# Hybrid decoder layer: three visits a head pair in the mixer, scores, transposes and PV in one stretch, norms in the transposes' PSUM banks

## The chip, the cores and the metric

One core of a Trainium2 chip runs one launch of the kernel. The metric is the device time of that launch in microseconds (us). Three runs of the kernel before gave 1025.48, 1026.85 and 1027.06 us; the median is 1026.85.

The names used below: PE is TensorE (matmuls and transposes; PEld its weight loads), DVE is VectorE, ACT is ScalarE, POOL is GpSimd, SP the queue that issues the loads.

## The reference

One decoder layer on 512 tokens of width 1024, in float32: a half-step SwiGLU FFN, a token mixer, a second half-step FFN, each behind an RMSNorm that is scaled and shifted by a conditioning vector. The change touches the mixer alone. It has eight stick-breaking heads and eight forgetting (fox) heads of width 64:

```python
# stick-breaking, for each tile of 128 queries
z = einsum('bhqd,bhkd->bhqk', q[start:end], k[:end]) * scale
mask = arange(end)[None, :] < arange(start, end)[:, None]
log_keep = where(mask, log_sigmoid(-z), 0)
later = cumsum(log_keep, reverse=True) - log_keep
w = where(mask, exp(log_sigmoid(z) + later), 0);  out = w @ v
# forgetting, with q and k RMS-normed per head (gains g_q, g_k)
z = z + log_f_cum[start:end, None] - log_f_cum[None, :end]
p = softmax(where(mask, z, -inf));  out = p @ v
```

log_f_cum is a running sum of log_sigmoid of a per-head forget gate. The heads are concatenated and multiplied by w_o.

## The kernel before, in words

Activations are held transposed (features on the partitions, 512 tokens along the row), with the tokens in reverse order, so that query tile i sees the last 512 - 128 i columns: tile 0 has 512 columns of scores, tile 3 has 128. To keep float32 precision, each operand of a projection is split into a high and a low part (`prep`, lines 119 to 124: ACT casts hi, and another engine subtracts to get lo), and each product is three matmuls (`mm3`, lines 126 to 129).

PSUM has eight banks of 128x512: three named mm (projections), two z (scores), two pt (transposes) and one o (the output of PV), line 106. A bank is given to a new tile when the last reader of the old one is done.

The mixer handles heads in pairs, `ORDER = [4, 5, 6, 7, 0, 1, 2, 3]`: four fox pairs, then four stick-breaking pairs. A pair's way:

- `project` (line 743) makes q and k of the pair, 8 steps of one `mm3` each. For a fox pair, the lo part of the second weight tile is made on POOL, everything else on DVE.
- For a fox pair `norm_start` (755) squares them on ACT and POOL (`nsq`, `nsh`, `nsl`), and `norm_end` (763) multiplies by a block of ones (`bones`, two matmuls) into an mm bank `m`. ACT then does Ln, Exp and a square on it (`rsqrt2`, 148), and DVE reads the bank in line 152 (`nu`), makes `nr` (153) and scales q or k (768, `nq`). Only after line 152 is the bank free.
- `stacks` (800) lays out QH, QL and KS for the scores.
- `scores` (817) does the score matmuls of one query tile i for the two heads into two z banks and then `weigh` (841): for fox a maximum and its correction on DVE (`mx`, 847 and 848), Exp on ACT (`fw`), a reciprocal on DVE (853), and the scaling on POOL (854); for stick-breaking two sigmoids on ACT (`keep`, `beta`), a scan on DVE (`R`, 861), and a product on POOL (864).
- `transposed` (867) transposes one head's weights, 128 columns at a time, into a pt bank and copies them out to PT; `values` (880) multiplies them with V into the o bank (PV); `heads_out` (892) splits the result.

Between these PE runs "filler": the projections of later pairs, V's projections (lines 598 to 628) and the first part of the output projection (`o_proj`), 181 steps of three to six matmuls. PE's order is the order in which the program is written (`manual_schedule` for PE); the orders on DVE, ACT and POOL are chosen by the scheduler. `advance(n)` (955) emits filler until n steps are done, and after each step it pops one entry of `side`, where the norms and the stacks wait for their turn. A pair's two norms are popped at the fourth and fifth step of the next pair's projection.

The main loop (966 to 982) goes over 32 units (pair, tile). Unit u emits its scores, filler up to `target(2u)`, the first head's transposes of unit u-1, one more step of filler, PV of unit u-2, filler up to `target(2u+1)`, and the second head's transposes of u-1. `target` is 36 + 2.5 t until t = 52, and then grows by 1.125 a half unit.

Of the kernel before, what the change touches and what calls it, by code (L numbers as in the profile page):

```python
# [33 lines left out]
def hybrid_layer(  # L34
# [626 lines left out]
    nc.gpsimd.affine_select(
        out=free_sb[:, :P], in_=free_sb[:, :P], compare_op=ALU.is_gt, fill=1.0, base=0, pattern=[[1, P]],
        channel_multiplier=-1,
    )
    nc.gpsimd.memset(keep_sb, 1.0)
    nc.gpsimd.affine_select(
        out=keep_sb[:, :P], in_=keep_sb[:, :P], compare_op=ALU.is_gt, fill=0.0, base=0, pattern=[[-1, P]],
        channel_multiplier=1,
    )
# [4 lines left out]
    logf = mp.tile([P, 8, 8], F32, tag="logf", name="logf")[:, :4, :]  # L674
    nc.vector.tensor_scalar(fneg, fc, -1.0, 0.0, op0=ALU.mult, op1=ALU.add)
# [87 lines left out]
    def norm_end(q, sh, sl, col):  # L763
        m = bank("mm")
        nc.tensor.matmul(m, bones, sh, start=True, stop=False)
        nc.tensor.matmul(m, bones, sl, start=False, stop=True)
# [49 lines left out]

    def scores(p, i):
        while p not in ready:
            side.pop(0)()
        KS, QH, QL = ST[p]  # L820
        fox = p >= NPAIR
        n = S - i * P
        nn = max(n, 256)
        zs = [bank("z") for _ in range(2)]
        qsl, ksl = slice(i * P, (i + 1) * P), slice(S - nn, S)
        for g, z in enumerate(zs):
            nc.tensor.matmul(z[:, :nn], QH[:, g, qsl], KS[:, g, ksl], start=True, stop=False)
# [3 lines left out]
        if not fox:  # L831
            for g, z in enumerate(zs):
                a, _ = halves(g)
                nc.tensor.matmul(z[:, :nn], QL[a, 0, qsl], KS[a, g, ksl], start=False, stop=True)
        return [weights(p, g, i, z[:, nn - n : nn], n) for g, z in enumerate(zs)]

    def weights(p, g, i, z, n):
        with tc.high_priority(offset=200):
            return weigh(p, g, i, z, n)

    def weigh(p, g, i, z, n):
        if p >= NPAIR:
            hd = 2 * (p - NPAIR) + g
            mx = mp.tile([P, 1], F32, tag="mx", name=nm("mx"), bufs=4)
            sm = mp.tile([P, 1], F32, tag="sm", name=nm("sm"), bufs=4)
            lq = lfq[:, i, hd : hd + 1]
            nc.vector.tensor_reduce(mx, z, AX.X, ALU.max)
            nc.vector.scalar_tensor_tensor(
                out=mx, in0=mx, scalar=lq, in1=lq, op0=ALU.add, op1=ALU.subtract, reverse1=True
            )  # L850
            w = wt2k("fw")
            act(w[:, :n], z, AF.Exp, bias=mx, accum_out=sm)
            nc.vector.reciprocal(sm, sm)
            nc.gpsimd.tensor_scalar(w[:, :n], w[:, :n], sm, 0.0, op0=ALU.mult, op1=ALU.add)
            return w, n
# [8 lines left out]
        nc.gpsimd.tensor_tensor(beta[:, :n], beta[:, :n], R[:, :n], op=ALU.mult)
        return beta, n

    def transposed(p, g, w, n):
        pt = bank("pt")
# [3 lines left out]
        if p < NPAIR:  # L872
            nc.vector.tensor_tensor(PT[:, :n], pt[:, :n], keep_sb[:, :n], op=ALU.mult)
        elif g:
            nc.scalar.copy(PT[:, :n], pt[:, :n])
        else:
            nc.vector.tensor_copy(PT[:, :n], pt[:, :n])
        return PT

    def values(p, i, pts, ob):  # L880
        n = 4 - i
        for j in range(n):
            for g in range(2):
                nc.tensor.matmul(  # L884
                    ob[g * 64 : g * 64 + 64, i * P : (i + 1) * P],
                    V[:, i + j, (2 * p + g) * 64 : (2 * p + g + 1) * 64],
                    pts[g][:, j * P : (j + 1) * P],
                    start=j == 0,
                    stop=j == n - 1,
                )  # L890

# [70 lines left out]

    units = [(p, i) for p in ORDER for i in range(4)]
    with tc.manual_schedule(engines={ENG.PE}):
        advance(36)
        ws, pts, obs = {}, {}, {}
        for u in range(len(units) + 3):
            if u < len(units):
                ws[u] = scores(*units[u])
            for g in range(2):  # L970
# [12 lines left out]
        advance(1000)  # L983
# [112 lines left out]
```

## Time and profile before

| what | us |
|---|---|
| median of three runs | 1026.85 |
| the profiled execution | 1026.44 |
| its span, first to last instruction | 1024.7 |
| mean granted PE clock | 0.993 of full |
| PE busy | 1004.2 |
| DVE busy | 576.3 |
| ACT busy | 373.1 |
| POOL busy | 125.7 |

The mixer takes roughly the stretch from 400 to 640 us. In a timeline a row gives the start, the time it took, the engine, the line, and the operation with `out<-in`, the tiles by the program's names. A mark such as `[3.86 <-DVE KS L795]` says that the engine stood idle for 3.86 us before this row and that DVE's write of KS in line 795 ended that. The granted clock is the share of full speed at which PE was allowed to run. Durations of PE's rows overlap, since matmuls are pipelined: what one costs is read from its start to the start of the next.

### The profile page before, as it was taken

To read this page: it belongs to the slowest core of one execution; us is meant where nothing else is said; L and a number is where in the kernel's file an instruction comes from. 1 tells how busy PE (TensorE), PEld (TensorE's weight loads), DVE (VectorE), ACT (ScalarE), POOL (GpSimd) and SP (SyncE) were. 2 spreads that over 40 slices of the span, in tenths; PEclk is the share of its full clock that TensorE was granted. 3 is DMA by queue.
4 is the path that set the end of the run, shared out by engine and by line. 5 is a ranking of instruction groups with operands and counts; after the bars stand their busy time and mean duration, and the time that the engine had idled before them with its cause. 6 is when DMAs were issued, how large, how long until landed. Compare 5 with 4: busy or idle time off the path is not lost.

```text
span 1024.7 us, 13165 instructions
## 1 busy us (share of the span) xinstructions
PE 1004.2 (98%) x5148; PEld 832.9 (81%) x5148; DVE 576.3 (56%) x942; ACT 373.1 (36%) x600; POOL 125.7 (12%) x125
## 2 busy tenths in 40 slices
PE   7999999999999999989999999999999999999998
PEld 6788888888888899767787767998888888888887
DVE  4999989534333447699867675753333333333332
ACT  5343212322222325767556461542222232123220
POOL 1000000000000123345313355100000000000000
PEclk8999999999999999989999999999999999999999
DMA  8889899432222312301111111232323322332221
GB/s 310 296 316 329 320 323 334 170 90 101 103 102 79 128 51 75 119 26 54 70 63 59 46 42 62 83 103 103 97 89 103 102 81 87 107 110 89 90 76 60
DMA packets 37357, 129.38 MB, mean 126 GB/s; under 512 B 4272, under 2 KB 4528, under 8 KB 37296
## 3 DMA queue, kind: packets, MB, share of 16 engines
q1 hardware_dynamic: 35856, 126.40, 36.1%
q10 hardware_dynamic: 1440, 2.16, 0.6%
q8 instruction: 40, 0.66, 0.3%
q14 instruction: 21, 0.17, 0.0%
HBM read 126.44 MB, written 2.10 MB: 125 GB/s over the span
## 4 chain that ended last, share of the span: by engine, by line
PE 84%; DVE 7%; issue 3%; DMA 2%; ACT 2%; POOL 1%; SPq 0%; ACTq 0%; DVEq 0%; POOLq 0%
PE mm L127 10%; PE mm L128 10%; PE mm L129 10%; PE pt L128 7%; PE pt L129 7%; PE pt L127 7%; PE z L128 6%; PE z L127 6%; PE z L129 6%; DMA wm<-wmod 2%; PE o L884 2%; PE pt L870 2%; PE mm L398 1%; DVE junk L211 1%; PE mm L607 1%
## 5 line engine op out<-in xcount | busy, mean ns | idle before, releaser
L122 ACT CAST hi<-raw 128x1024 fp32r<-128x1024 f32 (+2 forms) x154 | 158.8, 1033 | 450.7 <-PE mm L128 143.6
L123 DVE TENSOR_TENSOR lo<-raw,hi 128x1024 fp32r<-128x1024 f32 (+2 forms) x149 | 181.0, 1217 | 131.3 <-ACT hi L122 125.5
L127 PE MATMUL mm<-hh,hi 128*128 128x512 f32 (+1 forms) x464 | 183.5, 395 | 0.5 <-DVE nu L152 0.5
L128 PE MATMUL mm<-hl,hi 128*128 128x512 f32 (+1 forms) x464 | 178.0, 384 | 0.1
L129 PE MATMUL mm<-hh,lo 128*128 128x512 f32 (+1 forms) x464 | 178.0, 384 | 0.0
L128 PE MATMUL pt<-al,hi 128*128 128x512 f32 (+1 forms) x331 | 128.1, 387 | 0.3 <-DVE al L451 0.3
L129 PE MATMUL pt<-ah,lo 128*128 128x512 f32 (+1 forms) x331 | 128.0, 387 | 0.0
L127 PE MATMUL pt<-ah,hi 128*128 128x512 f32 (+1 forms) x331 | 128.0, 387 | 0.0
L128 PE MATMUL z<-hl,hi 128*128 128x512 f32 (+1 forms) x336 | 127.3, 379 | 0.0
L129 PE MATMUL z<-hh,lo 128*128 128x512 f32 (+1 forms) x336 | 127.3, 379 | 0.0
L127 PE MATMUL z<-hh,hi 128*128 128x512 f32 (+1 forms) x336 | 127.3, 379 | 0.0
L127 PEld LDWEIGHTS mm<-hh,hi 128*128 128x128 f32 x464 | 87.7, 189 | 19.8 <-issue 3.6
L129 PEld LDWEIGHTS mm<-hh,lo 128*128 128x128 f32 x464 | 87.5, 189 | 17.4
L462 DVE SCALAR_TENSOR_TENSOR x<-pt,gcol,x 128x512 f32<-128x512 f32 (+1 forms) x51 | 36.4, 713 | 114.5 <-PE pt L129 114.5
L128 PEld LDWEIGHTS mm<-hl,hi 128*128 128x128 f32 x464 | 87.7, 189 | 15.1 <-DVE hl L167 0.3
L447 DVE TENSOR_TENSOR av<-sg,z 128x512 f32<-128x512 f32 x41 | 28.1, 686 | 105.3 <-PE z L129 105.3
L211 DVE SCALAR_TENSOR_TENSOR junk<-wm,c_bc 128x1024 f32<-128x1024 f32 x56 | 68.4, 1221 | 10.8 <-DMA wm<-wmod 10.4
L128 PEld LDWEIGHTS pt<-al,hi 128*128 128x128 f32 x331 | 62.1, 188 | 13.2 <-DVE al L451 0.7
L127 PEld LDWEIGHTS z<-hh,hi 128*128 128x128 f32 x336 | 63.2, 188 | 11.9
L129 PEld LDWEIGHTS z<-hh,lo 128*128 128x128 f32 x336 | 63.2, 188 | 11.8
L128 PEld LDWEIGHTS z<-hl,hi 128*128 128x128 f32 x336 | 63.2, 188 | 11.8
L127 PEld LDWEIGHTS pt<-ah,hi 128*128 128x128 f32 x331 | 62.2, 188 | 12.8
(296 smaller groups left out, 1433.8 us busy)
## 6 DMA issues: line engine op xcount, KB each, us to landing
raw<-w SPq DMA_DIRECT2D x80, 512.0 KB, 3.5
wm<-wmod SPq DMA_DIRECT2D x72, 512.0 KB, 6.0
raw<-wqk SPq DMA_DIRECT2D x16, 512.0 KB, 3.5
raw<-w1d SPq DMA_DIRECT2D x16, 448.0 KB, 3.3
raw<-w2d SPq DMA_DIRECT2D x16, 448.0 KB, 3.2
raw<-w1s SPq DMA_DIRECT2D x8, 512.0 KB, 6.9
raw<-w1d SPq DMA_DIRECT2D x8, 512.0 KB, 5.1
raw<-wo SPq DMA_DIRECT2D x8, 512.0 KB, 3.4
```

What stands on the lines that cost most here:

```text
L122: nc.scalar.copy(hi, raw)
L123: (lo_engine or nc.vector).tensor_tensor(lo, raw, hi.bitcast(F32), op=ALU.subtract)
L127: nc.tensor.matmul(ps, lh, rh, start=first, stop=False)
L128: nc.tensor.matmul(ps, lh, rl, start=False, stop=False)
L129: nc.tensor.matmul(ps, ll, rh, start=False, stop=last)
L211: nc.vector.scalar_tensor_tensor(out=junk, in0=wm, scalar=1.0, in1=c_bc, op0=ALU.mult, op1=ALU.mult, accum_out=mods[:, i : i + 1])
L398: nc.tensor.matmul(kb[j], lh if n < 2 else ll, h["l" if n == 1 else "h"][k], start=False, stop=k == KD - 1 and n == 2)
L447: nc.vector.tensor_tensor(av, sg, ps[1], op=ALU.mult)
L462: nc.vector.scalar_tensor_tensor(out=x[e][:, sl], in0=ps[:, sl], scalar=g_col(gm)[:, e : e + 1], in1=x[e][:, sl], op0=ALU.mult, op1=ALU.add)
L607: nc.tensor.matmul(b[:, :n], hh, wh, start=k == 0, stop=False)
L870: nc.tensor.transpose(pt[:, j * P : (j + 1) * P], w[:, j * P : (j + 1) * P], ident)
L884: nc.tensor.matmul(ob[g * 64 : g * 64 + 64, i * P : (i + 1) * P], V[:, i + j, (2 * p + g) * 64 : (2 * p + g + 1) * 64], pts[g][:, j * P : ...
```

## The change

The mixer goes over 24 visits instead of 32 units: for each pair tile 0, tile 1, and then tiles 3 and 2 together in one z bank each (`VISITS`). Per visit PE's order is now one stretch: scores of this visit, both heads' transposes of the visit before, PV of the visit before that. Filler comes only between stretches, up to `target(v)`: 36 + 20 v / 3, and from v = 19.5 on 3 steps a visit. Within fox scores the masks' matmuls come last. `norm_end` takes its bank from pt instead of mm. The lo part of the second weight tile of a fox pair is made on DVE instead of POOL. `free_sb` and `keep_sb` become 640 columns wide so that a merged visit finds a mask for two blocks; the merged fox visit does maximum, Exp, reciprocal and scaling for each of its two blocks, and the merged stick-breaking visit one scan, one product and two sigmoids over 384 columns a head. `fcol` and `logf` share a tile, and `mx` and `sm` share a tile with eight buffers.

The core of the diff:

```diff
-    def target(t):
-        return int(min(36 + 2.5 * t, 163 + 1.125 * (t - 52)))
+    def target(v):
+        return int(min(36 + 20 * v / 3, 163 + 3 * (v - 19.5)))
+
+    VISITS = ((0,), (1,), (3, 2))
...
-            wt = prep(wqk[2 * p + u], D, nc.gpsimd if fox and u else None)
+            wt = prep(wqk[2 * p + u], D)
...
     def norm_end(q, sh, sl, col):
-        m = bank("mm")
+        m = bank("pt")
...
+        def mm(z, sl, w, r, **kw):
+            nc.tensor.matmul(z[:, sl], w, r, skip_group_check=len(seg) > 1, **kw)
+
         for g, z in enumerate(zs):
-            nc.tensor.matmul(z[:, :nn], QH[:, g, qsl], KS[:, g, ksl], start=True, stop=False)
+            for n, (i, _, sl, qsl, ksl) in enumerate(parts):
+                mm(z, sl, QH[:, g, qsl], KS[:, g, ksl], start=n == 0, stop=False)
             if fox:
-                nc.tensor.matmul(z[:, :nn], QL[:, g, qsl], late[p % 2][:, g, ksl], start=False, stop=False)
-                nc.tensor.matmul(z[:, nn - n : nn - n + P], ident_b, mask_fx, start=False, stop=True)
...
+                for i, _, sl, qsl, ksl in parts:
+                    mm(z, sl, QL[:, g, qsl], late[p % 2][:, g, ksl], start=False, stop=False)
+        if fox:
+            for z in zs:
+                for i, n, sl, _, _ in parts:
+                    mm(z, slice(sl.stop - n, sl.stop - n + P), ident_b, mask_fx, start=False, stop=True)
+        else:
+            for i, _, sl, qsl, ksl in parts:
+                for g, z in enumerate(zs):
+                    a, _ = halves(g)
+                    mm(z, sl, QL[a, 0, qsl], KS[a, g, ksl], start=False, stop=True)
...
-    units = [(p, i) for p in ORDER for i in range(4)]
+    units = [(p, seg) for p in ORDER for seg in VISITS]
     with tc.manual_schedule(engines={ENG.PE}):
-        advance(36)
         ws, pts, obs = {}, {}, {}
-        for u in range(len(units) + 3):
+        for u in range(len(units) + 2):
+            advance(target(u))
             if u < len(units):
                 ws[u] = scores(*units[u])
-            for g in range(2):
-                advance(target(2 * u + g))
-                if 0 <= u - 1 < len(units):
-                    p, i = units[u - 1]
-                    pts[p, i, g] = transposed(p, g, *ws[u - 1][g])
-                if g == 0 and 0 <= u - 2 < len(units):
-                    advance(target(2 * u) + 1)
-                    p, i = units[u - 2]
-                    if i == 0:
-                        obs[p] = bank("o")
-                    values(p, i, (pts.pop((p, i, 0)), pts.pop((p, i, 1))), obs[p])
-                    if i == 3:
-                        heads_out(p, obs.pop(p))
+            if 0 <= u - 1 < len(units):
+                pts[u - 1] = [transposed(units[u - 1][0], g, *ws[u - 1][g]) for g in range(2)]
+            if 0 <= u - 2 < len(units):
+                p, seg = units[u - 2]
+                if seg == VISITS[0]:
+                    obs[p] = bank("o")
+                values(p, pts.pop(u - 2), obs[p])
+                if seg == VISITS[-1]:
+                    heads_out(p, obs.pop(p))
```

Three places of the instructions' order show what moved. First, PE at the norms of the last fox pair (`nsh`, `nsl` are the squares' parts, `mm_` and `pt_` the banks). Before, this stands between the norm of k and the next transposes:

```order
L765 MATMUL mm_4150<-nsh_4066,bones 128x512
L766 MATMUL mm_4150<-nsl_4067,bones 128x512
L127 MATMUL mm_4078<-hh_2834,hi_4073 128x512
L128 MATMUL mm_4078<-hl_2842,hi_4073 128x512
L129 MATMUL mm_4078<-hh_2834,lo_4074 128x512
L127 MATMUL mm_4078<-hh_2835,hi_4073 128x512
L128 MATMUL mm_4078<-hl_2843,hi_4073 128x512
L129 MATMUL mm_4078<-hh_2835,lo_4074 128x512
L870 MATMUL pt_4178<-ident,fw_4049 128x128 x2
```

and now the sixth visit (visit 5, counted from 0) follows the norm of k at once:

```order
L768 MATMUL pt_4062<-nsh_4023,bones 128x512
L769 MATMUL pt_4062<-nsl_4024,bones 128x512
L835 MATMUL z_4073<-KS_3659,QH_3660 128x256 x2
L835 MATMUL z_4073<-k_602_3360,QL_3661 128x256 x2
L835 MATMUL z_4074<-KS_3659,QH_3660 128x256 x2
L835 MATMUL z_4074<-k_602_3360,QL_3661 128x256 x2
L835 LDWEIGHTS ident_b
L835 MATMUL z_4073<-mask_fx,ident_b 128x128
...
L894 MATMUL pt_4113<-ident,fw_3977 128x128 x3
L894 MATMUL pt_4119<-ident,fw_3984 128x128 x3
```

The norm's tile is pt_4062 now, and pt_4119, the second head's transposes, is given the same bank; the transposes of the first head get the bank of q's norm.

Second, DVE at the same place (`mx` is the maximum of the scores `z`, `nu` the read that frees a norm's bank). Before, the two reads stand with one copy between them, and the next scores' maxima behind both:

```order
L152 SCALAR_TENSOR_TENSOR nu_4110<-mm_4106,nu_4110 128x512
L853 RECIPROCAL sm_4132<-sm_4132 128x1
L853 RECIPROCAL sm_4140<-sm_4140 128x1
L153 SCALAR_TENSOR_TENSOR nr_4109<-nu_4110,nr_4109 128x512
L768 SCALAR_TENSOR_TENSOR nq_3939<-nq_3939,gs,nr_4109 128x512
L877 COPY PT_4181<-pt_4178 128x256
L152 SCALAR_TENSOR_TENSOR nu_4154<-mm_4150,nu_4154 128x512
L781 TENSOR_TENSOR QL_4166<-nq_3939,QH_4165 64x512
L153 SCALAR_TENSOR_TENSOR nr_4153<-nu_4154,nr_4153 128x512
L847 TENSOR_REDUCE mx_4221<-z_4213 128x1
```

and now, with z_4073 and z_4074 the scores of visit 5:

```order
L152 SCALAR_TENSOR_TENSOR nu_4052<-pt_4048,nu_4052 128x512
L871 TENSOR_REDUCE mx_4088<-z_4073 128x1
L153 SCALAR_TENSOR_TENSOR nr_4051<-nu_4052,nr_4051 128x512
L872 SCALAR_TENSOR_TENSOR mx_4088<-mx_4088,lfq 128x1
L771 SCALAR_TENSOR_TENSOR nq_3890<-nq_3890,gs,nr_4051 128x512
L876 RECIPROCAL mx_4088<-mx_4088 128x1
L871 TENSOR_REDUCE mx_4094<-z_4073 128x1
L871 TENSOR_REDUCE mx_4101<-z_4074 128x1
L872 SCALAR_TENSOR_TENSOR mx_4094<-mx_4094,lfq 128x1
L872 SCALAR_TENSOR_TENSOR mx_4101<-mx_4101,lfq 128x1
L152 SCALAR_TENSOR_TENSOR nu_4066<-pt_4062,nu_4066 128x512
```

The read of k's bank pt_4062 stands behind three maxima of visit 5's own scores and a reciprocal that needs ACT's Exp of them. At visits 1 and 3 it stands behind that visit's two maxima in the same way (rows `mx_3712`, `mx_3719`, then `nu_3649`; `mx_3910`, `mx_3917`, then `nu_3863`).

Third, POOL ahead of the first scores (`fw`, the first of them, is the scaling of visit 0's weights). Before:

```order
L123 TENSOR_TENSOR lo_3411<-raw_3409,hi_3410 128x1024
L123 TENSOR_TENSOR lo_3547<-raw_3545,hi_3546 128x1024
L760 TENSOR_TENSOR nsl_3404<-nsq_3402,nsh_3403 128x512
L123 TENSOR_TENSOR lo_3712<-raw_3710,hi_3711 128x1024
L760 TENSOR_TENSOR nsl_3443<-nsq_3441,nsh_3442 128x512
L760 TENSOR_TENSOR nsl_3531<-nsq_3529,nsh_3530 128x512
L123 TENSOR_TENSOR lo_3956<-raw_3954,hi_3955 128x1024
L760 TENSOR_TENSOR nsl_3582<-nsq_3580,nsh_3581 128x512
L854 TENSOR_SCALAR fw_3629<-fw_3629,sm_3626 128x512
```

and now:

```order
L763 TENSOR_TENSOR nsl_3407<-nsq_3405,nsh_3406 128x512
L763 TENSOR_TENSOR nsl_3446<-nsq_3444,nsh_3445 128x512
L763 TENSOR_TENSOR nsl_3534<-nsq_3532,nsh_3533 128x512
L763 TENSOR_TENSOR nsl_3585<-nsq_3583,nsh_3584 128x512
L877 TENSOR_SCALAR fw_3628<-fw_3628,mx_3629 128x512
```

The four casts of 1024 columns are in DVE's queue now, each behind ACT's cast of its hi part.

More of the change, by code (lines that the diff above doesn't have):

```diff
@@ L587, in hybrid_layer @@
     V = mp.tile([P, 4, D], F32, tag="V", name="V")
-    fcol = mp.tile([P, 8, 8], F32, tag="fcol", name="fcol")[:, :4, :]
+    fl32 = mp.tile([P, 8, 8], F32, tag="fl32", name="fl32")
+    fcol, logf = fl32[:, :4, :], fl32[:, 4:, :]
     evn = [0]
@@ L656, in hybrid_layer @@
         nc.vector.memset(bones.bitcast(F32)[g * 64 : (g + 1) * 64, g * 64 : (g + 1) * 64], 1.0 / 64)
-    free_sb = mconst([P, S], BF16, "free_sb")
-    keep_sb = mconst([P, S], BF16, "keep_sb")
+    free_sb = mconst([P, S + P], BF16, "free_sb")
+    keep_sb = mconst([P, S + P], BF16, "keep_sb")
     nc.gpsimd.memset(free_sb, 0.0)
[L661 to L664, printed above, removed]
     nc.gpsimd.memset(keep_sb, 1.0)
[L666 to L669, printed above, removed]
+    for blk in (slice(0, P), slice(P, 2 * P)):
+        nc.gpsimd.affine_select(
+            out=free_sb[:, blk], in_=free_sb[:, blk], compare_op=ALU.is_gt, fill=1.0, base=0, pattern=[[1, P]],
+            channel_multiplier=-1,
+        )
+        nc.gpsimd.affine_select(
+            out=keep_sb[:, blk], in_=keep_sb[:, blk], compare_op=ALU.is_gt, fill=0.0, base=0, pattern=[[-1, P]],
+            channel_multiplier=1,
+        )
     fc = fcol.rearrange("p s e -> p (s e)")
@@ L815, in stacks, with scores @@
         )
-    def scores(p, i):
+    def scores(p, seg):
         while p not in ready:
@@ L831, in scores @@
[L831 to L837, printed above, removed]
+                for i, _, sl, qsl, ksl in parts:
[9 more added lines that the diff above has]
+                    mm(z, sl, QL[a, 0, qsl], KS[a, g, ksl], start=False, stop=True)
@@ L838, in weights, with weigh @@
+        cut, at = [], 0
+        for i, n, _, _, _ in parts:
+            cut.append((i, n, at))
+            at += n
+        return [weights(p, g, cut, z[:, lo:off], at) for g, z in enumerate(zs)]
+    def weights(*args):
         with tc.high_priority(offset=200):
-            return weigh(p, g, i, z, n)
-    def weigh(p, g, i, z, n):
+            return weigh(*args)
+    def weigh(p, g, cut, z, n):
         if p >= NPAIR:
             hd = 2 * (p - NPAIR) + g
[L844 to L850, printed above, removed]
-            w = wt2k("fw")
[L852 to L855, printed above, removed]
+            w = wt2k("fw")
+            for i, m, at in cut:
+                sl = slice(at, at + m)
+                col = mp.tile([P, 2], F32, tag="mx", name=nm("mx"), bufs=8)
+                mx, sm = col[:, 0:1], col[:, 1:2]
+                lq = lfq[:, i, hd : hd + 1]
+                nc.vector.tensor_reduce(mx, z[:, sl], AX.X, ALU.max)
+                nc.vector.scalar_tensor_tensor(
+                    out=mx, in0=mx, scalar=lq, in1=lq, op0=ALU.add, op1=ALU.subtract, reverse1=True
+                )
+                act(w[:, sl], z[:, sl], AF.Exp, bias=mx, accum_out=sm)
+                nc.vector.reciprocal(sm, sm)
+                nc.gpsimd.tensor_scalar(w[:, sl], w[:, sl], sm, 0.0, op0=ALU.mult, op1=ALU.add)
+            return w, n, cut
@@ L860, in weigh, with transposed @@
         rti[0] += 1
+        f0 = 0 if len(cut) > 1 else P
         nc.vector.tensor_tensor_scan(
-            R[:, 1:n], keep[:, : n - 1], free_sb[:, : n - 1], 1.0, op0=ALU.mult, op1=ALU.max
+            R[:, 1:n], keep[:, : n - 1], free_sb[:, f0 : f0 + n - 1], 1.0, op0=ALU.mult, op1=ALU.max
         )
         nc.gpsimd.tensor_tensor(beta[:, :n], beta[:, :n], R[:, :n], op=ALU.mult)
-        return beta, n
-    def transposed(p, g, w, n):
+        return beta, n, cut
+    def transposed(p, g, w, n, cut):
         pt = bank("pt")
@@ L872, in transposed @@
         if p < NPAIR:
[L873 removed]
+            f0 = 0 if len(cut) > 1 else P
+            nc.vector.tensor_tensor(PT[:, :n], pt[:, :n], keep_sb[:, f0 : f0 + n], op=ALU.mult)
         elif g:
@@ L877, in transposed, with values @@
             nc.vector.tensor_copy(PT[:, :n], pt[:, :n])
[L878 to L882, printed above, removed]
-            for g in range(2):
[L884 to L890, printed above, removed]
+        return PT, cut
+    def values(p, pts, ob):
+        for i, m, at in pts[0][1]:
+            n = m // P
+            for j in range(n):
+                for g in range(2):
+                    nc.tensor.matmul(
+                        ob[g * 64 : g * 64 + 64, i * P : (i + 1) * P],
+                        V[:, i + j, (2 * p + g) * 64 : (2 * p + g + 1) * 64],
+                        pts[g][0][:, at + j * P : at + (j + 1) * P],
+                        start=j == 0,
+                        stop=j == n - 1,
+                    )
     def heads_out(p, ob):
```

12 lines of the change are left out of this document (7 added, 5 removed).

## The prediction

> **What bounds the kernel now.** I read the page first, then TensorE's waits in the mixer, then stretches of time with the granted clock, then the timelines.
>
> ```profile
> PE 1004.2 (98%) x5148; PEld 832.9 (81%) x5148; DVE 576.3 (56%) x942; ACT 373.1 (36%) x600; POOL 125.7 (12%) x125
> ```
>
> TensorE (PE) is busy 98% of the span and no other engine more than 56%. So only two things move the time: how long TensorE's own stream takes, and how long it stands. The change touches the mixer alone, 400 to 640 us. There TensorE's waits are these (engine, tile, line, what it waited for: us in total, times, longest):
>
> ```profile
> PE z L827 <- DVE KS L795: 3.9, 1, 3.9
> PE mm L607 <- DVE V L594: 1.3, 1, 1.3
> PE o L884 <- ACT PT L875: 1.3, 1, 1.3
> PE mm L766 <- POOL nsl L760: 1.0, 1, 1.0
> PE mm L127 <- DVE nu L152: 0.5, 1, 0.5
> PE z L607 <- DVE fcol L614: 0.5, 1, 0.5
> PE pt L870 <- POOL beta L864: 0.3, 1, 0.3
> ```
>
> Each happens once; together under 9 us. Standing has a second price, the clock (stretch, its length, busy us and count of PE, PEld, DVE, ACT, POOL, granted clock, DMA):
>
> ```profile
> 438.72:442.13 3.41, 0.75 (x4) 0.29 (x2) 3.35 (x4) 3.18 (x6) 2.51 (x2) 1.00 0.41 145
> 442.13:448.95 6.82, 5.62 (x14) 4.08 (x15) 5.64 (x12) 2.18 (x7) 0.98 (x1) 0.50 0.01 5
> ...
> 476.26:479.67 3.41, 2.15 (x11) 1.24 (x10) 3.29 (x6) 2.63 (x7) 2.42 (x3) 1.00 0.02 5
> ```
>
> The 3.9 us wait left TensorE 0.75 us busy in a 3.41 us stretch, and then it was granted half its clock for 6.82 us. The 1.3 us wait at 477 us (2.15 busy of 3.41) cost no clock. Somewhere between 1.3 and 2.7 us of standing in one such stretch the clock goes.
>
> **TensorE's own work.** One PV between two filler matmuls, four transposes and a stick-breaking score unit of 256 columns, and a PV of four matmuls (start, us, what):
>
> ```profile
> 483.80 0.40 PE L129 MATMUL mm<-hh,lo 128*128 128x512 f32 x1
> 484.13 1.09 PE L884 MATMUL o<-PT,V 128*64 128x128 f32 x16
> 485.15 0.50 PE L127 MATMUL mm<-hh,hi 128*128 128x512 f32 x1
> 485.50 0.40 PE L128 MATMUL mm<-hl,hi 128*128 128x512 f32 x1
> 485.74 0.40 PE L129 MATMUL mm<-hh,lo 128*128 128x512 f32 x1
> ...
> 597.59 0.66 PE L870 MATMUL pt<-ident,beta 128*128 128x128 f32 x4
> 598.00 0.48 PE L827 MATMUL z<-KS,QH 128*128 128x256 f32 x2
> 598.41 0.38 PE L834 MATMUL z<-KS,QL 64*128 64x256 f32 x2
> 598.72 0.50 PE L127 MATMUL mm<-oh,hi 128*128 128x512 f32 x1
> 599.06 0.39 PE L128 MATMUL mm<-ol,hi 128*128 128x512 f32 x1
> ...
> 626.18 0.44 PE L884 MATMUL o<-PT,V 128*64 128x128 f32 x4
> 626.55 0.50 PE L127 MATMUL mm<-ohl,hi 128*128 128x512 f32 x1
> ```
>
> I measure from start to start, since the durations overlap. A filler matmul takes 0.24 (485.50 to 485.74). The one ahead of PV takes 0.33, the one behind it 0.35: 0.09 + 0.11 for going in and out. Sixteen PV matmuls take 1.02, four 0.37, so 0.054 each and 0.15 fixed. A visit of PV has thus 0.35 us that do not depend on its length. 32 visits become 24: 8 x 0.35 = 2.8 us saved.
>
> A stick-breaking score unit of 256 columns takes 0.41 + 0.31 and 0.10 on the matmul behind it, 0.82; two of them 1.64. (The four transposes ahead of it take 0.41, 0.1 each.) Merged, four KS and four QL matmuls go in and out once. I put that at 1.25 (between 1.0 and 1.5), 0.4 less, on four pairs 1.6 us.
>
> Nothing is paid for the wider masks free_sb and keep_sb: GpSimd, 12% busy, makes them long before the stick-breaking visits, the second half of the mixer, read them; without that lead their two extra selects would stand ahead of the first of those scans.
>
> The rest (two masks behind each other rather than each between float32 matmuls, transposes that lead straight into PV, scores straight into transposes) the trace does not show. The count of matmuls stays. Bounds: nothing, or all of PV's 0.09 and half its 0.11 in 24 visits and about as much again at masks, 4 us. I take 1.5, nearer the low end, since PV still switches from whole-array to half-array matmuls. Sum: 2.8 + 1.6 + 1.5 = 5.9 us, from 4 to 8.5.
>
> **The first scores.** GpSimd (POOL) loses four casts to VectorE (DVE). Ahead of the first scores they stood in each other's way:
>
> ```profile
> 433.73 0.67 DVE L781 TENSOR_TENSOR QL<-nq,QH 64x512 fp32r<-64x512 f32 x1
> ...
> 437.25 2.93 DVE L781 TENSOR_TENSOR QL<-nq,QH 64x512 fp32r<-64x512 f32 x1
> 440.22 1.38 DVE L784 CAST QH<-QH 64x512 fp32r<-64x512 f32 x1
> ```
>
> ```profile
> 437.24 2.40 POOL L123 TENSOR_TENSOR lo<-raw,hi 128x1024 fp32r<-128x1024 f32 x1 [1.08 <-ACT hi L122]
> ```
>
> The same VectorE step took 0.67 alone and 2.93 when GpSimd's cast of 2.40 began beside it. With that cast gone 2.3 us leave the chain to KS; the cast of 1.38 may shrink too, one of the two sel casts is placed behind KS, and the head of the chain starts a little earlier because GpSimd reaches the norm's nsl sooner. (The Trainium skill, "SBUF — State Buffer", on the port pair that VectorE and GpSimd share, says that the one that starts second waits for the whole of the other's instruction; the trace agrees, 2.93 is 0.67 and most of 2.40.) The 1.0 (nsl) and the 0.5 (norm in the mm banks) go too, so TensorE also arrives 1.5 us sooner; what counts is when KS is ready. I take scores 0 to end 4 us earlier than in before. Low end 1: the moved casts now stand in VectorE's queue. High end 6: the half-clock stretch goes as well.
>
> The 1.3 us wait of PV for ACT's PT goes, since a copy now has a whole visit's filler in front of PV; so does the 0.3. The 1.3 at V's evacuation stays: the copy stands behind the next scores' reductions and ol as before. Saved in all: 5.9 + 4.0 + 1.6 = 11.5 us.
>
> **What the change adds.** A norm's bank is held from its first matmul until VectorE's nu has read it. Before, it was an mm bank, and only a filler group stood behind it (0.5 us). Now it is one of the two pt banks, and the next transposes stand behind it, and behind them in TensorE's queue PV and all filler. For the last fox pair's k (PE row, then DVE rows, then ACT rows):
>
> ```profile
> 488.18 0.40 PE L765 MATMUL mm<-nsh,bones 128*128 128x512 f32 x1
> ```
>
> ```profile
> 491.77 0.69 DVE L152 SCALAR_TENSOR_TENSOR nu<-mm,nu 128x512 f32<-128x512 f32 x1
> ...
> 493.61 1.29 DVE L847 TENSOR_REDUCE mx<-z 128x1 f32<-128x512 f32 x2
> 494.81 0.34 DVE L848 SCALAR_TENSOR_TENSOR mx<-mx,lfq 128x1 f32<-128x1 f32 x2
> ```
>
> ```profile
> 489.73 0.68 ACT L102 ACTIVATE nr<-mm,eps_t 128x512 f32<-128x512 f32 x1
> 490.44 0.63 ACT L102 ACTIVATE nr<-nr 128x512 f32<-128x512 f32 x1
> 491.11 0.63 ACT L151 ACTIVATE nu<-nr 128x512 f32<-128x512 f32 x1
> ```
>
> The bank was held from 488.18 to 492.46, 4.3 us. After it three visits come too soon, those that have a norm of k between the scores before and their own transposes; the second head's transposes take its bank.
>
> At visit 1 there are 5 filler steps (15 x 0.23) and scores of about 1 us behind the norm. At visit 3 there are 3 steps, at visit 5 none. By the hold alone the waits would be 0, 0.3 and 2.0 us (visit 5: norm 2 x 0.23, scores 1.4, first head's three transposes 0.3, so the bank is wanted 2.3 us after the norm's start): 2.3 us, the low bound.
>
> But in VectorE's new order nu of k stands behind both reductions of the visit's own scores, which end just ahead of the transposes. From the end of scores that is 1.29 + 0.34 + 0.69 = 2.3, and the first head's transposes (four, 0.4) run in the meantime: 1.9 to 2.3 at visit 1 (2.1), and at visit 3 (three transposes, 0.3) 2.0 to 2.6 (2.2). At visit 5 a reciprocal that waits for the scores' exponential stands there too, and ACT makes that only after q's and k's steps. Ln, Exp and square of k follow the same of q: 6 x 0.65 from 0.9 before the scores start, so 3.0 after it. Then come nu's 0.69, two small steps (0.34), two reductions over 384 columns together (1.29 for 1024 above, so an estimate of 0.7 with two starts) and the short exponential with its reciprocal (0.7, estimated from the 0.68 of Ln over 512 columns): about 2.5. The bank comes 5.5 us after the scores' start and is wanted at 1.8: 3.7. Sum 8.0 us, at most 9. I take the high end, since the order of the queue leaves no way round it.
>
> Two of the mm waits grow: without transposes between them, V's second and third group follow each other through one bank (0.6 for ACT's copy), and at the second V chunk a bank waits for QL behind two scans (0.7): 1.3 us, from 0.3 to 2.5.
>
> The tail: GpSimd's two products take 3.46 us.
>
> ```profile
> 609.71 3.46 POOL L864 TENSOR_TENSOR beta<-beta,R 128x512 f32<-128x512 f32 x2 [3.12 <-ACT beta L102]
> ```
>
> In before they ended at 613.17, and the first head's transposes had just been waited for (the 0.3 us at pt). Both heads now come at once, three steps after the scores instead of 3.4 and 4.5: 0.3 to 1 us of waiting in each of the last three visits, 1.5 us in all (0 to 3).
>
> The clock: visits 1, 3 and 5 leave TensorE standing 2.1, 2.2 and 3.7 us; the row of 0.75 busy shows that 2.7 suffice, the row of 2.15 that 1.3 do not. The last should lose the clock, one of the others as well. A half-clock stretch of 3.4 to 6.8 us loses 1.7 to 3.4, less what TensorE would have waited in it anyway: 2 x 2.2 = 4.4 us.
>
> Added: 8.0 + 1.3 + 1.5 + 4.4 = 15.2. Net 15.2 - 11.5 = +3.7. The profiled execution took 1026.44 us (span 1024.7), the median of the three runs is 1026.85; so 1030.1, say **1030**.
>
> **Rivals.**
>
> *The banks come free in time* (faster). If nu is not held back and the 4.3 us hold is all, the waits are 2.3 us and no clock is lost: 1026.44 - 11.5 + 2.3 + 1.3 + 1.5 = 1020.0. For it: the hold of before was measured among the same neighbours. Against: the order. It decides at visit 3: a wait there under 0.5 us. Chance 0.2.
>
> *The waits come, the clock holds.* Each wait may be split by a boundary of the clock's stretches: 1026.44 - 11.5 + 10.8 = 1025.7. Chance 0.1.
>
> *The clock is lost once, at visit 5 alone.* 1025.7 + 2.2 = 1027.9, chance 0.1. (The Trainium skill, "TensorE: Matmul & The Clock Gate", section "Why this matters for your kernels", asks for no gaps of more than about 3 us; by that rule this would be the case, and it speaks against the change. Here a stretch with 2.7 us of standing lost the clock, so the rule's edge is not sharp.)
>
> *The casts delay the first scores.* VectorE was busy without a break from 430 to 445 us; with the casts in that queue the gain of 4.0 is eaten: 1030.1 + 4.0 = 1034.1. Chance 0.1.
>
> The forecast keeps 0.5, with 1027 to 1034 as its own range.
>
> **Numbers.** Two runs of this kernel differ by up to 0.15%; 0.2%, 2 us, is about what can be told from no change. Faster: the first rival and a little of the second, 0.23. Same: the rest of the two clock rivals and the forecast's low edge, 0.22. Slower 0.55. The range 1020 to 1037 leaves out half the first rival and the ends where two clock losses of 3.4 us or a slow VectorE add up.
>
> **What would show it.** Right: TensorE's waits at transposes for nu, once each at three visits, about 2, 2 and 4 us; half clock after the last; scores 0 about 4 us earlier, with a wait for KS under 3; PV in 24 visits. Wrong: no waits for nu at pt; clock 1.00 all through the mixer; or the wait for KS at 4 us or more.

## The result and the profile after

The changed kernel took 1033.59 us (median of four runs, 1032.10 to 1034.82) beside 1026.45 for the kernel before (its three runs and a fourth): a ratio of 1.0071, 95% interval 1.0059 to 1.0084, slower by 7.1 us. The profiled execution took 1034.82 us, its span is 1032.9. Every trace below is one execution, up to 2.8 us off the median of its kernel, and the mean granted clock differs between executions of one kernel too (0.993 to 0.997 in before, 0.990 to 0.993 in after), so what a trace says of the clock holds for that execution.

The first part of the changed kernel's page (busy time, share, instructions):

```profile
PE 1002.1 (97%) x5148; PEld 838.2 (81%) x5148; DVE 579.6 (56%) x926; ACT 371.4 (36%) x580; POOL 107.2 (10%) x115
```

TensorE is busy 2.1 us less than before, and the span is 8.2 us longer: the loss is standing time. To locate it I take the same stretch of PE's stream in every kernel, the 1596 matmuls from the start that follows the 0.47 us wait in V's first projections to the end before the short wait in the next FFN. It is the whole of the mixer that the change reaches. Of before and of after (stretch, its length, busy us and count of PE, PEld, DVE, ACT, POOL, granted clock, DMA):

```profile
399.93:659.38 259.45, 251.25 (x1596) 200.18 (x1596) 186.52 (x342) 144.97 (x296) 103.44 (x95) 0.99 0.19 65
```

```profile
401.23:667.57 266.34, 249.28 (x1596) 205.70 (x1596) 189.87 (x325) 143.37 (x276) 84.86 (x85) 0.97 0.19 63
```

Length less busy is standing: 8.20 before, 17.06 after. The stretch is 6.9 us longer, 8.9 more standing and 2.0 less busy. (The other 1.3 us of the span lie ahead of the stretch. Its start varies over all the runs between 398.1 and 402.2 us, and follows no edit: it is 398.1 in two kernels that have the change's loop too.) TensorE's waits after, by what ended them:

```profile
PE pt L894 <- DVE nu L152: 7.6, 4, 2.5
PE pt L894 <- DVE PT L902: 3.1, 2, 2.7
PE z L835 <- DVE KS L798: 3.0, 2, 1.7
PE pt L894 <- POOL beta L888: 0.8, 1, 0.8
PE mm L608 <- DVE V L595: 0.7, 1, 0.7
PE pt L769 <- POOL nsl L763: 0.7, 1, 0.7
PE mm L608 <- ACT V L597: 0.5, 1, 0.5
```

The waits for nu are those that were forecast, at visits 1, 3 and 5 (the last two rows are visit 5, the first and the second head's transposes). Below them stand DVE's rows of visit 5, with nu of k behind the maxima:

```profile
452.76 0.63 PE L894 MATMUL pt<-ident,fw 128*128 128x128 f32 x4 [1.57 <-DVE nu L152]
...
475.30 0.52 PE L894 MATMUL pt<-ident,fw 128*128 128x128 f32 x3 [2.38 <-DVE nu L152]
...
493.24 0.55 PE L894 MATMUL pt<-ident,fw 128*128 128x128 f32 x3 [1.16 <-DVE nu L152]
496.30 0.90 PE L894 MATMUL pt<-ident,fw 128*128 128x128 f32 x3 [2.51 <-DVE nu L152]
```

```profile
494.79 0.60 DVE L871 TENSOR_REDUCE mx<-z 128x1 f32<-128x256 f32 x2
495.31 0.34 DVE L872 SCALAR_TENSOR_TENSOR mx<-mx,lfq 128x1 f32<-128x1 f32 x2
495.56 0.68 DVE L152 SCALAR_TENSOR_TENSOR nu<-pt,nu 128x512 f32<-128x512 f32 x1
```

The second row of the waits, for DVE's PT, was not forecast. It is almost all visit 2: TensorE, then DVE and POOL at that place.

```profile
450.59 0.60 PE L894 MATMUL pt<-ident,fw 128*128 128x128 f32 x4
...
459.30 0.52 PE L894 MATMUL pt<-ident,fw 128*128 128x128 f32 x3
462.51 0.52 PE L894 MATMUL pt<-ident,fw 128*128 128x128 f32 x3 [2.70 <-DVE PT L902]
```

```profile
455.69 0.16 DVE L876 RECIPROCAL mx<-mx 128x1 f32<-128x1 f32 x1 [1.89 <-ACT fw L102]
...
457.40 0.69 DVE L784 TENSOR_TENSOR QL<-nq,QH 64x512 fp32r<-64x512 f32 x1
458.12 0.70 DVE L787 CAST QH<-QH 64x512 fp32r<-64x512 f32 x1
458.85 2.79 DVE L799 CAST k<-KS 64x512 fp32r<-64x512 f32 x2
461.68 0.69 DVE L902 COPY PT<-pt 128x512 f32<-128x512 f32 x1
```

```profile
458.63 2.73 POOL L798 TENSOR_TENSOR KS<-nq,KS 64x512 fp32r<-64x512 f32 x2
```

The copy at 461.68 empties the bank of the first head's transposes of the stretch before (the row at 450.59), and the second head's transposes at 462.51 need that bank. The data of the copy was there at 451.2. But DVE takes its instructions in their order: it even stood idle for 1.89 us up to 455.69, waiting for ACT, and did not do the copy. The copy stands in its order behind the stacks of the next pair, whose two casts take as long as POOL's KS beside them: 2.79 us, 1.4 each. The clock was lost three times (stretches as above):

```profile
440.34:443.75 3.41, 1.91 (x7) 1.09 (x8) 3.28 (x6) 2.57 (x5) 1.44 (x1) 1.00 0.00 0
443.75:447.16 3.41, 3.41 (x9) 2.69 (x9) 3.23 (x8) 1.15 (x3) 0.08 (x1) 0.50 0.42 147
460.82:464.23 3.41, 1.72 (x20) 1.41 (x21) 3.35 (x4) 1.39 (x3) 1.81 (x2) 1.00 0.03 7
464.23:467.64 3.41, 3.41 (x9) 2.65 (x9) 2.66 (x13) 1.37 (x6) 0.64 (x2) 0.50 0.44 154
471.06:474.47 3.41, 1.86 (x12) 1.21 (x10) 3.26 (x7) 3.35 (x6) 0.00 (x0) 1.00 0.00 0
491.54:494.95 3.41, 1.09 (x10) 0.64 (x8) 2.58 (x8) 3.17 (x8) 0.00 (x0) 1.00 0.42 154
494.95:501.78 6.83, 5.48 (x26) 4.24 (x27) 6.47 (x16) 4.07 (x11) 4.01 (x6) 0.50 0.00 0
```

That is at the first scores, at visit 2's wait for the copy, and at visit 5. The 2.4 us wait of visit 3 (471.06 to 474.47 holds 1.55 of it) cost no clock. Half clock: 13.7 us, in before 6.8.

### The profile page after: what moved, and what is told of

It is laid out like the page before. It is cut to its first block, busy times and chain, and to the rows that moved or that the text cites. A ratio compares the mean times of both kernels' runs of the same rounds, so it can differ in the third digit from the quotient of the medians.

```text
span 1032.9 us, 13064 instructions
## 1 busy us (share of the span) xinstructions
PE 1002.1 (97%) x5148; PEld 838.2 (81%) x5148; DVE 579.6 (56%) x926; ACT 371.4 (36%) x580; POOL 107.2 (10%) x115
## 4 chain that ended last, share of the span: by engine, by line
PE 81%; DVE 9%; issue 3%; DMA 3%; ACT 3%; POOL 1%; SPq 0%; DVEq 0%; POOLq 0%; ACTq 0%
PE mm L127 10%; PE mm L128 10%; PE mm L129 9%; PE pt L128 7%; PE pt L129 7%; PE pt L127 7%; PE z L128 6%; PE z L129 6%; PE z L127 6%; DMA wm<-wmod 2%; PE o L910 2%; PE mm L398 1%; PE z L835 1%; PE pt L894 1%; DVE lo L123 1%
## 5 line engine op out<-in xcount | busy, mean ns | idle before, releaser
L123 DVE TENSOR_TENSOR lo<-raw,hi 128x1024 fp32r<-128x1024 f32 (+2 forms) x153 | 185.2, 1212 | 143.3 <-ACT hi L122 137.5
L127 PE MATMUL mm<-hh,hi 128*128 128x512 f32 (+1 forms) x464 | 180.8, 390 | 0.0
```

Source lines behind the costliest of these rows:

```text
L123: (lo_engine or nc.vector).tensor_tensor(lo, raw, hi.bitcast(F32), op=ALU.subtract)
L127: nc.tensor.matmul(ps, lh, rh, start=first, stop=False)
```

## The experiments

The theory after the result: the norms in the pt banks are the loss, 7.6 us of waits and the clock. The rivals: the stretch (scores, both transposes and PV in one piece ask DVE for too much at once), and the casts on DVE. Four kernels separate them.

**Norms back in the mm banks**, all else as changed:

```diff
-        m = bank("pt")
+        m = bank("mm")
         nc.tensor.matmul(m, bones, sh, start=True, stop=False)
```

> The changed kernel with the norms' tiles back in the mm banks, all else as changed. Bank theory (the norms in pt banks are the loss: 7.6 us of waits for nu, and with them two or three half-clock stretches of about 2 us): 1033.6 - 7.6 - 4.4 = 1021.6 us, between 1019 and 1025, no PE wait for nu at the transposes, the 2.7 us wait for the PT copy at visit 2 stays or shrinks, half clock at most once or twice. Rival, the stretch (scores, both transposes and PV in one piece ask DVE for too much at once; the waits only take another name, PT or mm): 1029 to 1034. Rival, the casts on DVE are the loss: 1028 to 1031, since only part of the waits goes.

1031.2 us, ratio 1.0045 (1.0027 to 1.0063). The theory fell: only 2.4 of the 12 us that it expected came back. TensorE's waits at the transposes in that run:

```profile
PE pt L894 <- DVE PT L902: 3.4, 2, 2.0
PE pt L894 <- POOL fw L877: 2.5, 2, 2.3
PE pt L894 <- ACT PT L900: 1.4, 1, 1.4
```

No wait for nu is left there (one of 1.4 us is at an mm bank now), but 7.3 us of others stand in its place, and the clock was at half in 20.5 us. In this trace TensorE stands 4.0 us less than in after and is busy 2.9 us longer. Visit 4, on DVE:

```profile
477.16 0.82 DVE L787 CAST QH<-QH 64x512 fp32r<-64x512 f32 x1
478.01 1.37 DVE L799 CAST k<-KS 64x512 fp32r<-64x512 f32 x1
479.31 0.54 DVE L902 COPY PT<-pt 128x384 f32<-128x384 f32 x1
```

TensorE stood from 478.62 to 480.00 for that copy, again behind the stacks' casts.

**The casts back on POOL**, all else as changed:

```diff
-            wt = prep(wqk[2 * p + u], D)
+            wt = prep(wqk[2 * p + u], D, nc.gpsimd if fox and u else None)
```

> The changed kernel with the lo part of the second weight tile of a fox pair back on POOL, all else as changed. Bank theory: the waits for nu stay and the first scores come 1 to 3 us later: 1033 to 1036 us. Rival, the casts on DVE hold up the queue of maxima, nu and PT copies: 1026 to 1030. Rival, the stretch: 1033 to 1036, as the bank theory.

1035.46 us, 1.0088 (1.0072 to 1.0103). The rival of the casts falls: on POOL they are no better. The waits for nu and PT are the same (7.6 and 3.1), the wait for KS is 3.9 again.

**Both edits**, so that merged visits and stretch are left:

```diff
-            wt = prep(wqk[2 * p + u], D)
+            wt = prep(wqk[2 * p + u], D, nc.gpsimd if fox and u else None)
...
-        m = bank("pt")
+        m = bank("mm")
```

> The changed kernel with both the norms in mm banks and the casts on POOL: what is left is the merged visits and the stretch. Bank theory: own work of TensorE saves 5.9 us and nothing is lost but a wait or two: 1020 to 1025 us, 1 to 3 above the run with only the norms moved back, because the first scores wait longer for KS. Rival, the stretch: 1028 or more.

1036.78 us, 1.0092 (1.0074 to 1.0111). With the casts on POOL the norms' bank makes no difference that these runs tell (1.0088 and 1.0092), and the copies are later still:

```profile
PE pt L894 <- DVE PT L902: 7.8, 2, 4.7
PE z L835 <- DVE KS L798: 3.9, 1, 3.9
```

**The kernel before with the norms in pt**, that line alone:

```diff
-        m = bank("mm")
+        m = bank("pt")
```

> The kernel before with one edit: the norms' tiles in the pt banks. Bank theory: in the order of before only one or two norms stand close enough to the transposes that take their bank (the second fox pair's, one filler step and no scores between k's norm and the transposes that take q's bank): a wait of about 2 us for nu, perhaps a half-clock stretch: 1028 to 1031 us. Rival, that the bank of a norm does not matter by itself (the stretch makes it matter): 1026 to 1027.

1031.43 us, 1.0047 (1.0032 to 1.0062): a cost of its own, a little over what was expected.

```profile
465.76 0.50 PE L765 MATMUL pt<-nsh,bones 128*128 128x512 f32 x1 [0.90 <-DVE PT L877]
467.39 0.44 PE L870 MATMUL pt<-ident,fw 128*128 128x128 f32 x2 [0.89 <-DVE nu L152]
480.35 0.63 PE L870 MATMUL pt<-ident,fw 128*128 128x128 f32 x4 [2.25 <-DVE PT L877]
```

A norm in a pt bank takes the place of one head's transposes, so here too a copy becomes urgent.

The new theory: two things hold a pt bank too long, a norm until nu and a head's transposes until their copy, and either alone is enough to stop TensorE. The next three test the second and take merging and stretch apart; a fourth prices the casts alone.

**The copies first** in the engines' order, norms in mm banks:

```diff
-        if p < NPAIR:
-            f0 = 0 if len(cut) > 1 else P
...
+        with tc.high_priority(offset=200):
+            if p < NPAIR:
+                f0 = 0 if len(cut) > 1 else P
...
```

> The changed kernel with the norms in mm banks, and with the copies out of the transposes' banks (PT) given the same precedence in the engines' order as the weights, so that DVE does them ahead of the stacks' casts. New theory (the queue: the stretch asks at once for what DVE used to have a visit for, and the copies of PT stand in DVE's order behind casts that POOL's KS stretches by the shared port): the 3.4 us of waits for DVE's PT and the 1.4 for ACT's go, and with them two half-clock stretches of about 1.7 us: 1031.2 - 4.8 - 3.4 = 1023, between 1021 and 1026. Rival, DVE as a whole is the bound in the fox visits, in whatever order: the waits move to KS, fw or nu and the time stays at 1029 to 1033. Rival, the clock: the waits at POOL's fw keep the clock low anyway, 1027.

1023.77 us, 0.9972 (0.9961 to 0.9984): 7.4 less than without it, and faster than before. The waits for copies at the transposes are gone, and half clock remains in one stretch of 3.4 us, at the first scores. Between the two traces most of the gain is clock: TensorE stands 1.9 us less and is busy 6.4 us less for the same matmuls. What took the copies' place is this:

```profile
PE z L835 <- ACT fw L102: 4.6, 5, 1.6
```

The next scores wait for z banks that ACT's exponentials read, and the exponentials wait for DVE's maxima (ACT stood 2.24 us for them up to 463.50). The copies are only a small part of what stands ahead of the maxima: there one copy of 0.55 us, two casts of 0.42 and a weight cast of 1.21.

**Merging without the stretch**: three visits, norms in mm, the loop of before (first head's transposes, one step, PV, half a visit of filler, second head's transposes):

```diff
-        return int(min(36 + 20 * v / 3, 163 + 3 * (v - 19.5)))
+        return int(min(36 + 10 * v / 3, 163 + 1.5 * (v - 39)))
...
-            advance(target(u))
...
+            for g in range(2):
+                advance(target(2 * u + g))
```

> The changed kernel with the norms in mm banks and the loop's spread of before: three visits a pair, but the second head's transposes half a visit of filler after the first head's, and PV one filler step after the first head's, the scores after the second head's. Left of the change: merging and the casts on DVE. Queue theory: the merging itself gains (own work 4 to 5 us) and the spread gives DVE its time: 1020 to 1026. Rival, merging is the cost (a merged fox visit has four maxima, exponentials, reciprocals and scalings where it had two): 1029 to 1034, as with the stretch.

1027.91 us, 1.0012 (1.0002 to 1.0022). This lies between the two expectations, 1.9 above the one and 1.1 below its rival. With the copies as scheduled, spreading the visit gains 3.3 us over the stretch (1031.2). What is left is a copy again, 4.3 us at one place:

```profile
PE pt L894 <- DVE PT L902: 4.8, 2, 4.3
```

**The stretch without merging**, 5 steps a visit, norms in mm:

```diff
-        return int(min(36 + 20 * v / 3, 163 + 3 * (v - 19.5)))
+        return int(min(36 + 5 * v, 163 + 2.25 * (v - 26)))
...
-    VISITS = ((0,), (1,), (3, 2))
+    VISITS = ((0,), (1,), (2,), (3,))
```

> The changed kernel with the norms in mm banks and four visits a pair (tiles 0, 1, 2, 3), 5 filler steps a visit, scores, both transposes and PV in one stretch. Left of the change: the stretch and the casts on DVE. Queue theory: a visit is 3.5 us of filler long instead of 4.6, and the chain of weights has to fit into it: waits for PT and fw at least as long as with three visits, 1030 to 1036. Rival, merging is the cost: 1024 to 1027.

1048.24 us, 1.0210 (1.0184 to 1.0236), far over what was expected.

```profile
PE pt L894 <- DVE PT L902: 8.7, 2, 4.6
PE pt L894 <- ACT PT L900: 4.0, 2, 3.5
PE pt L894 <- POOL beta L888: 3.8, 4, 1.5
```

With 5 steps of filler a visit in place of 6.7, copies and weights come later. Within the stretch the merged visits are thus 17 us faster than the unmerged ones (1031.2 against 1048.24).

**The kernel before with the casts on DVE**, that line alone:

```diff
-            wt = prep(wqk[2 * p + u], D, nc.gpsimd if fox and u else None)
+            wt = prep(wqk[2 * p + u], D)
```

> The kernel before with one edit: the lo part of the second weight tile of a fox pair on DVE. By the two pairs of runs so far (1033.6 against 1035.5 with the casts on POOL, 1031.2 against 1036.8) the casts on DVE gain 2 to 5 us in the changed kernel: here 1021 to 1025 us, with the waits for KS under 3 us and those for nsl and nu of 1.0 and 0.5 gone. Rival, the casts help only where the stretch makes DVE late: 1026 to 1027.

1024.70 us, 0.9983 (0.9973 to 0.9992): they gain about 2 us by themselves. The wait for nsl is gone and those for the first scores' KS and k are 0.9 and 0.8; the wait for nu at an mm bank grew from 0.5 to 1.4. In the profiled execution no half clock is left in the mixer:

```profile
400.03:656.15 256.12, 249.33 (x1596) 198.56 (x1596) 186.09 (x345) 144.94 (x296) 92.50 (x91) 1.00 0.20 66
```

**The changed kernel with the copies first**, norms in pt (the diff of the copies alone). With this run the four cases of bank and order are complete:

> The changed kernel, norms in pt banks as changed, with one edit: the copies out of the transposes' banks (PT) first in the engines' order. It differs from the run that gave 1023.8 us in the norms' bank alone. If the order of DVE's queue is all of it: the wait of 2.7 us for PT goes and the waits for nu shrink to 2 to 4 us, 1024 to 1027. If the norms' bank is a cost of its own: waits for nu of 6 to 8 us at three visits and two half-clock stretches stay, 1029 to 1033.

1031.09 us, 1.0047 (1.0032 to 1.0062). The norms' bank is a cost of its own after all, once the copies are first: 7.3 us beside the 1023.77. But it does not show as the expected 6 to 8 us of waits for nu. Most of the waits have the copies' name:

```profile
PE pt L894 <- DVE PT L903: 5.4, 3, 3.0
...
PE pt L894 <- DVE nu L152: 2.3, 2, 1.2
```

TensorE at visit 3, then DVE:

```profile
470.05 0.52 PE L894 MATMUL pt<-ident,fw 128*128 128x128 f32 x3 [1.20 <-DVE nu L152]
473.56 0.87 PE L894 MATMUL pt<-ident,fw 128*128 128x128 f32 x3 [2.99 <-DVE PT L903]
```

```profile
472.86 0.55 DVE L903 COPY PT<-pt 128x384 f32<-128x384 f32 x1
473.33 0.68 DVE L152 SCALAR_TENSOR_TENSOR nu<-pt,nu 128x512 f32<-128x512 f32 x1
```

The second head's transposes start at 473.56, when the first head's copy has ended (473.41) and before nu has (474.01): k's norm still holds the other bank, and both heads go through one.

| changed kernel, ratio to before | copies as scheduled | copies first |
|---|---|---|
| norms in pt | 1.0071 | 1.0047 |
| norms in mm | 1.0045 | 0.9972 |

Each edit alone gives a quarter of what both give: 2.4 us for the bank, 2.5 for the copies, 9.8 for both.

**Merged, spread, copies first**, norms in mm (the loop's and the copies' diffs together):

> Three visits a pair, spread as before, norms in mm banks, casts on DVE, PT first in the engines' order. Beside the run of 1027.9 us the waits for PT of 4.8 and 0.8 us should go, and the two half-clock stretches with them (10.2 us at half clock, less 1.7 of standing in it: at most 4.3): 1027.9 - 5.6 - 4.3 = 1018.0, between 1017 and 1022. Rival, the stretch is no cost once PT comes first: no faster than the 1023.8 of the stretch with PT first, 1022 to 1025.

1025.05 us, 0.9984 (0.9970 to 0.9998). A miss by 7; the rival holds, the stretch is no cost once the copies are first (0.9972 with it). The wait for PT at the transposes went, the 0.8 at a PV stayed, and 6.8 of the 10.2 us of half clock are left. V's copy, now behind a copy of PT, took the place of the first:

```profile
PE mm L608 <- DVE V L595: 2.9, 1, 2.9
PE z L835 <- POOL fw L877: 2.3, 1, 2.3
```

**With the norms first too**:

```diff
-        r = rsqrt2(m, wt2k("nr"), wt2k("nu"))
+        with tc.high_priority(offset=200):
+            r = rsqrt2(m, wt2k("nr"), wt2k("nu"))
```

> As the run before it, with Ln, Exp, square and nu of the norms first in the engines' order too. The 1.4 us of an mm bank's wait for nu at 429 us should shrink: 0.5 to 1.5 us less than without it. Rival: what is put ahead delays the maxima and the weights: the same or 1 to 2 us more.

1026.00 us, 0.9993 (0.9983 to 1.0002): no gain, and the wait of 1.4 for nu at the mm bank is unchanged. In the trace it does not come from what stands ahead of nu on DVE: DVE stood idle for 1.19 us in front of it, for ACT's square. ACT began the norm's Ln at 428.25, 1.5 us after the norm's matmuls had ended (426.77), behind a cast for the forget gates (L718) that had itself waited 1.66 us for DVE's `fl`.

**KS on DVE**, on the kernel of 1023.77:

```diff
-            eng = nc.vector if p == ORDER[0] else nc.gpsimd
+            eng = nc.vector
```

> The run of 1023.8 us (three visits, stretch, norms in mm banks, PT first) with one edit: the subtractions of KS of the three later fox pairs on DVE instead of POOL. Beside POOL's KS the casts of 64x512 on DVE took 1.4 us each, alone 0.42. If that port is what makes the maxima and with them the exponentials late, the 4.6 us of waits of the scores' banks for ACT's exponentials shrink to 1 to 3 us: 1020 to 1023. Rival, DVE is simply full there, and the added 0.67 each makes up for the shorter casts: 1023 to 1026.

1023.57 us, 0.9970 (0.9960 to 0.9981): the same time. TensorE's waits for exponentials shrank from 4.6 to 2.3, as by the theory of the port, but it waits 1.6 for V's copy where it waited 0.5 and 1.4 for the weights' scaling where 0.8. Taking POOL's KS away moves the queue about and gains nothing that the runs tell. Its stretch, without half clock in the profiled execution:

```profile
401.79:656.69 254.90, 244.43 (x1596) 201.35 (x1596) 190.82 (x332) 142.65 (x276) 79.25 (x79) 1.00 0.21 66
```

All kernels over that stretch, read in the same way (half clock is the time at a granted clock of 0.50 in it):

| kernel | length | busy | standing | half clock |
|---|---|---|---|---|
| before | 259.45 | 251.25 | 8.20 | 6.8 |
| changed | 266.34 | 249.28 | 17.06 | 13.7 |
| norms in mm | 265.26 | 252.21 | 13.05 | 20.5 |
| casts on POOL | 269.28 | 250.29 | 18.99 | 17.1 |
| both | 270.75 | 251.17 | 19.58 | 17.1 |
| before, norms in pt | 265.31 | 254.85 | 10.46 | 13.7 |
| norms in mm, copies first | 256.92 | 245.78 | 11.14 | 3.4 |
| merged, spread | 261.38 | 248.50 | 12.88 | 10.2 |
| stretch, unmerged | 281.49 | 258.05 | 23.44 | 27.3 |
| before, casts on DVE | 256.12 | 249.33 | 6.79 | 0 |
| changed, copies first | 263.62 | 248.72 | 14.90 | 10.2 |
| merged, spread, copies first | 257.71 | 247.00 | 10.71 | 6.8 |
| the same, norms first | 257.26 | 245.51 | 11.75 | 3.4 |
| norms in mm, copies first, KS on DVE | 254.90 | 244.43 | 10.47 | 0 |

## Why the prediction was right in the time, and where not in the reason

The forecast was 3.7 us more, and 7.1 came. In the traces the mixer's stretch is 6.9 longer. By the terms of the forecast (us; own work and clock are worked out below, the rest are TensorE's waits of before and after):

| term | forecast | in the traces |
|---|---|---|
| TensorE's own work | -5.9 | -4.9 |
| up to the first scores | -4.0 | -2.4 |
| PV's wait for ACT's PT | -1.3 | -1.3 |
| nu | +8.0 | +7.6 |
| DVE's PT at the transposes | 0 | +3.1 |
| nsl at visit 5 | 0 | +0.7 |
| mm banks | +1.3 | +0.2 |
| tail, with the 0.3 at pt | +1.2 | +0.8 |
| clock | +4.4 | +2.9 |
| sum | +3.7 | +6.7 |

**TensorE's own work.** In the profiled executions two kernels held full clock over the whole stretch: before with the casts on DVE, unmerged, at 249.33 busy, and the merged one with KS on DVE at 244.43. That is 4.9 us for the same 1596 matmuls, within the forecast's bounds. That most of it is the merging and not the stretch shows at the merged, spread kernel with the norms first: 245.51, which is 3.8 less than unmerged even with its half-clock stretch left in.

**The waits for nu**, 7.6 in place of 8.0: 1.57 at visit 1 (2.1 forecast), 2.38 at visit 3 (2.2), 3.67 at visit 5 (3.7). The place, the order that causes it and the size were right. At visit 5 nu of k ended 5.5 us after the scores' start, as forecast; but 1.16 of the 3.67 already stand before the first head's transposes, for q's bank, which the forecast had free by then.

**The first scores**: TensorE stood 5.4 us up to them before (1.0, 0.5, 3.9) and 3.0 after (1.70 and 1.28, the wait for KS that was to be under 3). By the forecast's own measure, from the start of the stretch to the end of scores 0, it is 42.27 in place of 45.65, so 3.4 of the 4.0; the part that is not standing belongs in the main to the clock, since before ran these scores at half clock. The mm banks and the tail were overpriced: 1.5 in place of 1.3 at the V copies, and 0.8 more at the tail (0.83 + 0.24 less 0.28).

**The clock.** Busy above the full-clock kernels is 251.25 - 249.33 = 1.9 in before and 249.28 - 244.43 = 4.85 after, so 2.9 more. A half-clock stretch of 3.41 us costs less than the 2.2 forecast: by its rows (444.28 to 444.71, then 445.13) a matmul takes 0.43 from start to start where it takes 0.23 at full clock, so one that is full of them loses about 1.6 (an estimate); the two kernels with one such stretch are busy 1.35 and 1.08 above the 244.43. And visit 2 lost the clock as well as visit 5. The prediction's example of 2.7 us of standing was part of one wait of 3.86 us, so it did not show that shorter waits suffice; after does, with 1.5 us of standing in two waits (the stretch with 1.91 busy).

**The step that failed** is "The 1.3 us wait of PV for ACT's PT goes, since a copy now has a whole visit's filler in front of PV". It is true of PV. But the same copies also free the banks of the next transposes, which now come both at once, and DVE does not do a copy when its data is there but when its turn comes: at visit 2 the data was there at 451.2 and the copy began at 461.68. The 3.1 us for PT, which the sum put at nothing, and a half-clock stretch come from that. That the time still came out inside the range is in part luck: the overpriced clock, mm banks, tail and nu made room for these waits.

**The reason.** The prediction put the loss on the norms' bank. Its first rival leaves 2.3 of the 8.0 us of waits and no loss of clock, and gives 1020.0. With the norms back in mm, and no wait for nu left at the transposes, the time is 1031.2: the copies' waits, partly hidden by nu's, come out, with more half clock. Shown: bank and order of the copies together make 9.8 us, neither alone more than 2.5. The rival that the casts delay the first scores is wrong in its sign; on DVE they gain 2 us in the kernel before, and 5.6 in the kernel with the norms in mm.

**Left open.** The copies were not put first in the kernel before, so how much of the 1023.77 is merging and how much the order is not settled. It is not told apart from the 1024.70 of the kernel before with the casts on DVE alone: the intervals of the ratios overlap (0.9961 to 0.9984 and 0.9973 to 0.9992), and over the mixer's stretch its trace is 0.8 us longer (256.92 against 256.12). Merging saves 4.9 of work there and pays 4.4 of it back in standing (11.14 against 6.79) and 1.35 in clock. So that merging gains anything over before with the casts moved is not shown.

## What to carry to other kernels

When a change shortens the time between a result and its use, list everything that holds a buffer in between and read in the order of the engine that frees it what stands ahead. A wait that the trace names hides the next one in the queue: price its removal by what is late next, and undo two suspects together as well as one by one. Before merging work for fewer switches of TensorE, give the copies that free its banks precedence: here the same saving of 4.9 us ended at +7.1 us without that, and at -3.3 with it and the norms in other banks, of which the casts alone give 2.4 in the kernel before.

## What the runs showed of the hardware

The clock can go without a long gap: in after no wait of TensorE in the mixer was over 2.70 us, and the stretches of 3.41 us that cost it had TensorE busy for 1.91, 1.72 and 1.09; one with 1.86 busy (471.06 to 474.47) kept it. In the other runs one with 2.04 busy lost it (441.05 to 444.46 with the norms first) and one with 1.64 kept it (463.31 to 466.72 with merged, spread, copies first). So busy time alone does not mark the edge, and what does is not settled. The Trainium skill, "TensorE: Matmul & The Clock Gate", section "Part 1: The HAM clock gate (the "warmup" mystery)", puts the drop after one idle window of about 3.4 us; the length agrees with the 3.41 of the rows, but the windows here were half busy, and the measurement decides.

DVE's casts of 64x512 took 0.42 alone and 1.4 beside POOL's subtraction of KS. Yet without POOL's part the time stayed the same, 1023.57 against 1023.77: here the lengthened casts cost no time that the runs tell, since other waits took the place of those that went.
